# Gates and two parts of the short convolution by rows, norms spread through DRAM, and first loads on two queues

## The chip, the core and the metric

The kernel runs on one core of a Trainium2 chip. The core has five engines with an instruction queue each: TensorE (PE in the profile; its weight loads, PEld, overlap its matmuls), VectorE (DVE), ScalarE (ACT), GpSimd (POOL) and SyncE (SP). Each takes its own queue in order. DMA transfers are issued from the queues of SP, ACT and POOL. The metric is device time of one execution in microseconds, lower is better.

## What is computed

One block of a hybrid encoder on 256 tokens of width 2048, in float32: a norm, one projection w_in into four mixers (gated linear attention, an FFT mixer, long convolutions, a short convolution), their outputs normed and projected by w_out, then cross-attention to 256 memory tokens and a gated MLP of inner width 5632. Cut to what the change touches:

```python
def short_conv(u, w):
    up = jnp.pad(u, ((0, 0), (1, 1), (0, 0)))
    return up[:, :-2] * w[0] + up[:, 1:-1] * w[1] + up[:, 2:] * w[2]

def shortconv_mixer(u, conv_w):
    b, c, h = jnp.split(u, 3, axis=-1)
    return b * short_conv(c * h, conv_w)

def gla_mixer(q, k, v, g, lr, gk_w, gk_b, norm_g):
    ...
    o = rms_norm(o, norm_g) * jax.nn.silu(heads(g, GLA_DV))

def reference(...):
    mem_n = rms_norm(mem, mem_norm_g)
    h = rms_norm(x, norm_g[l, 0])
    q, k, v, g, lr, u_f, u_h, u_s = jnp.split(h @ w_in[l], split_at, axis=-1)
    y_a = gla_mixer(q, k, v, g, lr, ...)
    y_b = rms_norm(fnet_mixer(u_f), grp_norm_g[l, 0])
    y_c = rms_norm(hyena_mixer(u_h, ...), grp_norm_g[l, 1])
    y_d = rms_norm(shortconv_mixer(u_s, sc_conv_w[l]), grp_norm_g[l, 2])
    x = x + jnp.concatenate([y_a, y_b, y_c, y_d], axis=-1) @ w_out[l]
    x = x + cross_attention(rms_norm(x, norm_g[l, 1]), mem_n, w_xq[l], w_xkv[l], w_xo[l])
    x = x + swiglu(rms_norm(x, norm_g[l, 2]), w_gate_up[l], w_down[l])
```

## The kernel before

**Weights and precision.** All weights stream once from DRAM, as blocks of 128 x 128, sixteen to a slab of 1 MB, in the very order in which the matmuls use them. Each half slab (eight blocks) is split on the way: ScalarE casts it to the high part wh (line 104), VectorE subtracts it from the raw one and makes the low part wl (line 105). Activations are split the same way into 512 columns, 256 high and 256 low. A product is wh x (high, low) plus wl x high, all in the matrix engine's fast float32 form. `Stream.take` (from line 110) gives out the blocks and keeps two to three halves ready ahead; SP's queue loads the slabs (line 83). Before the very first slab is in, `st.after` hands out other loads between the slabs' pieces, one after each.

**Three forms of a product.** `gemm` with `mm` yields *features*: 128 output columns on the partitions and the 256 tokens along the free axis; a block costs a matmul of 512 columns (L298) and one of 256 (L299). Its two halves have to be added afterwards (`merge`, L305). The *narrow* form of `mm` takes three matmuls of 256 (L295, L296, L299) and needs no merge. `gemm_rows` with `part_rows` yields *rows*: tokens on the partitions, 512 output columns along the free axis; four blocks cost six matmuls of 512 (L347 to L349). What is computed by rows but wanted as features is turned: VectorE transposes blocks of 32 x 32 (`store_turned`, L382), POOL's queue stores them to DRAM, and `load_turned` (L389) reads them back so that rows and columns change places; the features then stand in a turned order, which the host puts into the weights that use them.

**Side work.** Everything but the big products is written as generators in `Background`. After each product step `poll` takes a step of those that are due by a count of PE time and of VectorE's debts; `yield` without a number pauses a generator by 1.3 us plus the debt, SOON by almost nothing, FAR by 18 us. `drain` forces a generator to its end at once. The instructions of each engine are put in order at build time by a planner, which can put an instruction ahead of others that were written earlier when it takes the engine to be free; `keep_place` forbids that.

**The stages around the change.** First the keys and values of memory, by rows, with memory's slices scaled as they arrive (`start_m`). Beside it `prepare` sums the squares of memory and x, gets the reciprocal root as a column (`rstd_cols`) and spreads it along the free axis: `rstd_end` scales an identity by it (L275), and a matmul with ones (L282) puts it on all partitions, copied to krs (L285). x's row rsx is used by `start_x`, which norms and splits x's slices (L204 and L200); memory's row rsm scales the attention's scores. After memory the filters of the long convolution are computed (`filters`, with `dft`, L1069). Then w_in: twelve feature columns for the long convolution, v by rows, k and q by features, the first three short convolution columns narrow, FNet by rows, the other nine short convolution columns by features, the four gates narrow. In the background GLA's `mix`, FNet's `mix` and the short convolution's `group_norm` go on. `out_proj` takes the inner dimension in four parts, the long convolution's, GLA's, the short convolution's and FNet's; ahead of each but the first it drains the generator concerned and issues loads of x for the residual. Attention and the MLP follow; the MLP's first Silu (L870) closes the first pair of gate and up.

Small tiles of 256 columns come from a pool of eleven (`tmp`); PSUM has four banks for the big products (pg) and four for side work (pm).

## Time and profile before

| | us |
|---|---|
| median of 3 runs | 1478.01 |
| lowest and highest | 1476.25 and 1478.46 |
| profiled execution, its own time | 1477.61 |
| its span, first to last instruction | 1475.6 |
| PE busy in the span | 1463.1 |
| VectorE, ScalarE, POOL busy | 930.6, 754.5, 152.9 |

The span's rest to the execution's time, 2.0 us, lies around it. In the rows that follow, a timeline row gives start, duration, engine, line and operation, output and input, and in brackets the engine's idle time before it with what ended it; starts and durations are in us from the span's start. The matmuls' durations are modelled and overlap, so a matmul of 512 columns shows 0.39 while the next starts 0.23 later.

### The profile page before, as it was taken

The numbers are of one execution on the slowest core, as the hardware profiler recorded it, in microseconds if no ns is written. First come the engines' busy times: TensorE is split into PE (matmuls) and PEld (weight loads), VectorE is DVE, ScalarE is ACT, GpSimd is POOL, SyncE is SP. The second block draws the span as 40 slices with busy tenths as digits, with TensorE's granted clock in tenths as the row PEclk, the third lists the DMA queues.
The fourth block names the chain that finished last, engine by engine and source line by source line (L and its number), as shares of the span: only waits on it lengthen the run. The fifth ranks groups of instructions, "written<-read, shape, count | busy, mean of one in ns | idle before, by whom it ended". The sixth has DMA issues, their size and how long they took to land.

```text
span 1475.6 us, 18641 instructions
## 1 busy us (share of the span) xinstructions
PE 1463.1 (99%) x7068; PEld 1227.5 (83%) x7068; DVE 930.6 (63%) x1336; ACT 754.5 (51%) x1104; POOL 152.9 (10%) x204
## 2 busy tenths in 40 slices
PE   9999999999999999999999999999999999999997
PEld 7887888898898888888888888888888888888886
DVE  6668768778777575886765554555555456444445
ACT  6557655467556463665544444444444445434344
POOL 0000100000001223420501100111100111000000
PEclk9999999999999999999999999999999999999999
DMA  9776655454536777764857666666666666555554
GB/s 355 272 282 243 208 206 171 145 182 168 200 129 205 232 260 236 248 190 143 260 197 218 207 216 214 227 215 217 226 214 206 215 219 229 189 186 195 199 198 144
DMA packets 57146, 312.33 MB, mean 212 GB/s; under 512 B 8381, under 2 KB 10078, under 8 KB 25440
## 3 DMA queue, kind: packets, MB, share of 16 engines
q1 hardware_dynamic: 46352, 281.11, 55.3%
q0 software_dynamic: 10272, 29.37, 7.3%
q8 instruction: 55, 0.90, 0.2%
q10 hardware_dynamic: 432, 0.66, 0.1%
q14 instruction: 35, 0.29, 0.1%
HBM read 294.33 MB, written 16.78 MB: 211 GB/s over the span
## 4 chain that ended last, share of the span: by engine, by line
PE 97%; DVE 1%; ACT 0%; DMA 0%; issue 0%; SPq 0%; DVEq 0%
PE pg L347 24%; PE pg L349 24%; PE pg L348 24%; PE pg L298 9%; PE pg L299 6%; PE pm L349 1%; PE pm L348 1%; PE pm L347 1%; PE pg L295 1%; PE pg L296 1%; PE pm L1069 1%; PE pm L843 1%; PE pm L815 0%; DMA raw<-in_W 0%; PE pm L1450 0%
## 5 line engine op out<-in xcount | busy, mean ns | idle before, releaser
L105 DVE TENSOR_TENSOR wl<-raw,wh 128x1024 fp32r<-128x1024 f32 (+2 forms) x505 | 611.6, 1213 | 464.3 <-ACT wh L104 462.9
L104 ACT CAST wh<-raw 128x1024 fp32r<-128x1024 f32 (+2 forms) x505 | 523.9, 1039 | 567.8 <-PE pg L349 469.3
L347 PE MATMUL pg<-wh,act 128*128 128x512 f32 (+1 forms) x1434 | 559.7, 390 | 1.6 <-ACT wh L104 1.2
L348 PE MATMUL pg<-wl,act 128*128 128x512 f32 (+1 forms) x1434 | 558.0, 389 | 0.6 <-DVE wl L105 0.5
L349 PE MATMUL pg<-wh,act 128*128 128x512 f32 (+1 forms) x1434 | 558.0, 389 | 0.0
L347 PEld LDWEIGHTS pg<-wh,act 128*128 128x128 f32 x1434 | 269.2, 188 | 59.8 <-ACT wh L104 1.8
L348 PEld LDWEIGHTS pg<-wl,act 128*128 128x128 f32 x1434 | 269.2, 188 | 56.6 <-DVE wl L105 1.4
L349 PEld LDWEIGHTS pg<-wh,act 128*128 128x128 f32 x1434 | 269.2, 188 | 56.1
L298 PE MATMUL pg<-act,wh 128*128 128x512 f32 x576 | 202.9, 394 | 0.0
L299 PE MATMUL pg<-act,wl 128*128 128x256 f32 x688 | 192.7, 280 | 0.0
L299 PEld LDWEIGHTS pg<-act,wl 128*128 128x128 f32 x688 | 129.4, 188 | 0.4
L298 PEld LDWEIGHTS pg<-act,wh 128*128 128x128 f32 x576 | 108.2, 188 | 23.5
L384 POOL DMA_DIRECT2D hidden<-u x22 | 16.7, 762 | 403.3 <-DVE u L382 403.3
L347 PE MATMUL pg<-wh,f 128*128 128x512 f32 x120 | 46.7, 389 | 0.0
L348 PE MATMUL pg<-wl,f 128*128 128x512 f32 x120 | 46.7, 389 | 0.0
L349 PE MATMUL pg<-wh,f 128*128 128x512 f32 x120 | 46.7, 389 | 0.0
L389 POOL DMA_DIRECT2D tmp<-hidden x44 | 38.8, 888 | 46.7 <-DMA hidden<-u 29.6
L295 PE MATMUL pg<-act,wh 128*128 128x256 f32 x112 | 31.7, 283 | 0.0
L296 PE MATMUL pg<-act,wh 128*128 128x256 f32 x112 | 31.4, 281 | 0.0
L389 POOL DMA_DIRECT2D mr<-keys x16 | 14.1, 888 | 152.2 <-DVE act L200 148.1
L348 PEld LDWEIGHTS pg<-wl,f 128*128 128x128 f32 x120 | 22.5, 188 | 4.7
L347 PEld LDWEIGHTS pg<-wh,f 128*128 128x128 f32 x120 | 22.5, 188 | 4.7
(311 smaller groups left out, 1198.4 us busy)
## 6 DMA issues: line engine op xcount, KB each, us to landing
raw<-in_W SPq DMA_DIRECT2D x246, 1024.0 KB, 5.0
raw<-in_W SPq DMA_DIRECT2D x11, 512.0 KB, 7.3
hidden<-u POOLq DMA_DIRECT2D x22, 256.0 KB, 3.6
tmp<-hidden POOLq DMA_DIRECT2D x44, 128.0 KB, 4.3
features<-tmp POOLq DMA_DIRECT2D x24, 128.0 KB, 3.2
res<-in_xT SPq DMA_DIRECT2D x5, 512.0 KB, 6.7
ar<-features POOLq DMA_DIRECT2D x20, 128.0 KB, 6.2
k<-in_mem SPq DMA_DIRECT2D x8, 256.0 KB, 8.4
```

The lines of the kernel that those rows point to most:

```text
L104: nc.scalar.copy(wh[:, a:b], r[:, a:b])
L105: nc.vector.tensor_tensor(out=wl[:, a:b], in0=r[:, a:b], in1=wh[:, a:b].bitcast(F32), op=ALU.subtract)
L295: self.nc.tensor.matmul(p[:, 0:R], wh, slot[:, 0:R], start=start, stop=False)
L296: self.nc.tensor.matmul(p[:, 0:R], wh, slot[:, R:512], start=False, stop=False)
L298: self.nc.tensor.matmul(p[:, :], wh, slot[:, :], start=start, stop=False)
L299: self.nc.tensor.matmul(p[:, 0:R], wl, slot[:, 0:R], start=False, stop=stop)
L347: self.nc.tensor.matmul(p, hi, wh, start=start, stop=False)
L348: self.nc.tensor.matmul(p, hi, wl, start=False, stop=False)
L349: self.nc.tensor.matmul(p, lo, wh, start=False, stop=stop)
L384: self.nc.gpsimd.dma_start(to[r], u.rearrange("p (k c) -> p k c", c=P))
L389: self.nc.gpsimd.dma_start(t.rearrange("p (g t) -> p g t", t=32), src)
L843: nc.tensor.matmul(p[:, :], vh[m][:, s], pt[m][:, :], start=m == 0, stop=False)
```

## The change

1. Gates and the parts c and h of the short convolution are computed by rows, 512 columns each, and their results (Silu of the gates, the product c x h) turned through DRAM by POOL's queue. Part b stays by features, now after the gates; no column is narrow any more. A new generator `short_conv` reads the products back, takes the taps, multiplies by b and norms.
2. FNet's projection moves ahead of them, into the stage before; `Fnet` is split into `__init__` and `open`.
3. `out_proj` takes FNet second, GLA third and the short convolution last.
4. `spread` replaces `rstd_end` for memory and x: POOL's queue stores the two columns to DRAM in token order, and a second transfer reads them back onto all partitions.
5. At the start, memory's slices 1 to 3 are issued from POOL's queue at once, instead of between the slabs' pieces on SP's.
6. One more `yield` ahead of each `dft` of the filters, and a Silu on one column in the MLP's `norm()`, kept in its place.
7. The host turns the weights, gains and taps that see the turned order.

```diff
@@ constants @@
-ROWS = ((0, 512), (704, 768), (880, 944), (1152, 1344), (1408, 1600), (1664, 1856), (1920, NBLK))
+ROWS = ((0, 512), (704, 768), (832, 1088), (1152, 1344), (1408, 1600), (1664, 1856), (1920, NBLK))
-NSC = 3
@@ -287,6 +285,15 @@
         return rest
+    def spread(self, y, pool):
+        n = next(self.kept)
+        d = self.nc.dram_tensor(f"spread{n}", (1, R), F32, kind="Internal").ap()
+        rs = pool.tile([P, R], F32, name=f"krs{n}")
+        self.nc.gpsimd.dma_start(d.rearrange("o (r p) -> p (o r)", p=P), y)
+        self.nc.gpsimd.dma_start(rs, d.partition_broadcast(P)[:, 0, :])
+        return rs
     def mm(self, p, w, k, c, slot, start, stop, narrow=False):
@@ -300,10 +307,10 @@
         self.bg.pe(0.353 if narrow else 0.346)
         self.bg.poll()
-    def merge(self, p):
+    def merge(self, p, u=None):
         t = self.tmp()
         self.nc.scalar.copy(t, p[:, R:512])
-        u = self.tmp()
+        u = self.tmp() if u is None else u
         self.tt(u, p[:, 0:R], t, ALU.add)
@@ -408,10 +415,11 @@
         self.xf = [self.outside(n, KT) for n in ("features1", "features2")]
         self.qf = self.outside("queries", KT)
+        self.sf, self.gf = self.outside("products", 4), self.outside("gates", 4)
         self.ff = self.outside("hidden", FT)
         self.vd = nc.dram_tensor("values", (P, 8 * 512), F32, kind="Internal").ap()
-        def load(src, k, n):
-            nc.sync.dma_start(self.res[k // 4][:, k % 4:k % 4 + n, :].rearrange("p k r -> p (k r)"),
+        def load(src, k, n, by=nc.sync):
+            by.dma_start(self.res[k // 4][:, k % 4:k % 4 + n, :].rearrange("p k r -> p (k r)"),
                               self.t[src][:, k * R:(k + n) * R])
@@ -423,8 +431,10 @@
         nc.vector.memset(self.eps, EPS)
         nc.scalar.copy(self.eps, self.eps)
-        st.after = [lambda: None, lambda: None]
-        st.after += [lambda a=a: load("memT", *a) for a in ((1, 1), (2, 1), (3, 1), (4, 1), (5, 1), (6, 2), (8, 2), (10, 2), (12, 2), (14, 2))]
+        for k in (1, 2, 3):
+            load("memT", k, 1, nc.gpsimd)
+        st.after = [lambda: None for _ in range(5)]
+        st.after += [lambda a=a: load("memT", *a) for a in ((4, 1), (5, 1), (6, 2), (8, 2), (10, 2), (12, 2), (14, 2))]
         st.after.append(lambda: nc.sync.dma_start(self.vec, self.t["vecs"]))
@@ -484,36 +494,33 @@
             self.rcm = self.rstd_cols(c[0][:, 0:2], D, self.cp)
             yield
-            rest = self.rstd_end(self.rcm, 0, self.cp)
-            yield
-            self.rsm = rest()
+            self.rsm = self.spread(self.rcm, self.cp)
             self.bg.add(hy.filters())
             nc.sync.dma_start(gl.lrw, self.t["lrw"])
             while not rows:
                 yield 3
             yield from squares("x", c[1])
-            rest = self.rstd_end(self.rstd_cols(c[1][:, 0:2], D), 0, mid)
-            yield
-            self.rsx = rest()
+            self.rsx = self.spread(self.rstd_cols(c[1][:, 0:2], D), mid)
         UF, UH, US = 1568, 2080, 3616
-        scols, cur = [], {}
-        for j in range(4):
-            scols += [US + 512 + j * P, US + 1024 + j * P, US + j * P]
-        def ev_s(i, p):
-            j, what = i // 3, i % 3
-            u = p[:, 0:R] if i < NSC else self.merge(p)
-            if what == 0:
-                cur["c"] = u
-                if i < NSC:
-                    cur["c"] = self.tmp()
-                    nc.scalar.copy(cur["c"], u)
-            elif what == 1:
-                self.tt(cur["c"], u, cur["c"], ALU.mult)
-                cur["y"] = self.conv3(cur["c"], V_SCW + 3 * j)
-            else:
-                self.tt(self.res[1][:, j, :], u, cur["y"], ALU.mult)
+        def short_conv(u0):
+            m = []
+            for k in range(4):
+                m.append(self.tmp())
+                self.load_turned(m[-1], self.sf, k)
+            yield FAR
+            for j in range(4):
+                m[j] = self.conv3(m[j], V_SCW + 3 * j)
+                yield
+            for j in range(4):
+                while len(u0) <= j:
+                    yield
+                y = self.res[1][:, j, :]
+                self.tt(y, y, m[j], ALU.mult)
+                yield SOON
+            yield from self.group_norm(self.res[1], 2, act[20:24])
         with tc.tile_pool(name="mid", bufs=1) as mid:
@@ -550,24 +557,41 @@
                     nc.scalar.copy(gl.v[r], p)
                 self.gemm("w_in", [256, 384, 0, 128], h, lambda i, p: gl.feed(i, self.merge(p)))
-                self.gemm("w_in", scols[0:NSC], h, ev_s, narrow=True)
+                fn = Fnet(self, act[20:24])
+                fn.feed(self.gemm_rows("w_in", [UF], h)[0])
                 self.bg.drain()
             with tc.tile_pool(name="glp", bufs=1) as glp:
                 gl.open(glp)
-                fn = Fnet(self, glp, act[20:24])
+                fn.open(glp)
                 g_gla = self.bg.add(gl.mix(act[4:8]))
-                fn.feed(self.gemm_rows("w_in", [UF], h)[0])
                 g_fn = self.bg.add(fn.mix(act[0:4], gl))
-                self.gemm("w_in", scols[NSC:], h, lambda i, p: ev_s(i + NSC, p))
-                g_sc = self.bg.add(self.group_norm(self.res[1], 2, act[20:24]), True)
-                def ev_gate(i, p):
-                    nc.scalar.activation(gl.gate[i], p[:, 0:R], AF.Silu)
-                self.gemm("w_in", [1024 + i * P for i in range(4)], h, ev_gate, narrow=True)
+                halves = [(r, j) for r in range(2) for j in range(0, 512, R)]
+                ps = self.gemm_rows("w_in", [US + 512], h)[0]
+                c = [self.tmp() for _ in halves]
+                for t, (r, j) in zip(c, halves):
+                    nc.scalar.copy(t, ps[r][:, j:j + R])
+                ps = self.gemm_rows("w_in", [US + 1024], h)[0]
+                for t, (r, j) in zip(c, halves):
+                    self.tt(t, ps[r][:, j:j + R], t, ALU.mult)
+                    self.store_turned(self.sf, j // P, r, self.tmp(), t)
+                u0 = []
+                g_sc = self.bg.add(short_conv(u0), True, True)
+                ps = self.gemm_rows("w_in", [1024], h)[0]
+                for r, j in halves:
+                    t = self.tmp()
+                    nc.scalar.activation(t, ps[r][:, j:j + R], AF.Silu)
+                    self.store_turned(self.gf, j // P, r, self.tmp(), t)
+                for k in range(4):
+                    self.load_turned(gl.gate[k], self.gf, k)
+                def ev_s(i, p):
+                    u0.append(i)
+                    self.merge(p, self.res[1][:, i, :])
+                self.gemm("w_in", [US + i * P for i in range(4)], h, ev_s)
                 gl.done = True
-                return self.out_proj(lambda n: self.bg.drain((g_gla, g_sc, g_fn)[n]))
+                return self.out_proj(lambda n: self.bg.drain((g_fn, g_gla, g_sc)[n]))
     def conv3(self, u, c, y=None):
@@ -675,7 +699,7 @@
             if n:
                 before(n - 1)
-                for c in ((2, 3), (1,), (0,))[n - 1]:
+                for c in ((0,), (2, 3), (1,))[n - 1]:
                     if c == 3:
@@ -684,7 +708,7 @@
         self.mix = act[4:8] + act[0:4] + act[16:24]
-        return self.gemm_rows("w_out", [0, 512], self.mix, parts=[range(k, k + 4) for k in (8, 0, 12, 4)], before=ready)
+        return self.gemm_rows("w_out", [0, 512], self.mix, parts=[range(k, k + 4) for k in (8, 4, 0, 12)], before=ready)
     def attention(self, ps):
@@ -893,6 +917,10 @@
                     yield pause
         def norm():
+            mark = self.mark()
+            nc.scalar.activation(self.mg[:, 0:1], self.mg[:, 0:1], AF.Silu)
+            self.keep_place(mark)
             yield 2.0
@@ -1164,6 +1192,7 @@
                     m.append(self.halves(d))
                     yield SOON
+                yield
                 self.dft(cs, m, self.sp[o][cs])
@@ -1418,8 +1447,11 @@
 class Fnet:
-    def __init__(self, b, pool, s):
+    def __init__(self, b, s):
         self.b, self.s = b, s
+    def open(self, pool):
+        b = self.b
         tile_ = lambda n, w: [pool.tile([P, w], F32R, name=n + x) for x in "hl"]
@@ kernel() @@
+    for a, n in ((V_GRP + 8, 4), (V_GLA, 1), (V_SCW, 12)):
+        vecs[:, a:a + n] = turned(vecs[:, a:a + n])
...
-    src["w_xq"][:, 1536:] = turned(src["w_xq"][:, 1536:].T).T
+    for n, a in (("w_xq", 1536), ("w_in", 512), ("w_in", 3616)):
+        src[n][:, a:a + 512] = turned(src[n][:, a:a + 512].T).T
+    for a in (0, 1536):
+        src["w_out"][a:a + 512] = turned(src["w_out"][a:a + 512])
```

More of the change, by code (lines that the diff above doesn't have):

```diff
@@ L1517 @@
     vecs[:, V_NG:V_NG + 48] = col(x["norm_g"])
-    for c in (16, 32):
-        vecs[:, V_NG + c:V_NG + c + 12] = turned(vecs[:, V_NG + c:V_NG + c + 12])
     vecs[:, V_GRP:V_GRP + 12] = col(x["grp_norm_g"])
@@ L1528 @@
     vecs[:, V_NT:V_NT + 2] = nt
+    for a, n in ((V_GRP + 8, 4), (V_GLA, 1), (V_SCW, 12)):
+        vecs[:, a:a + n] = turned(vecs[:, a:a + n])
+    for c in (16, 32):
+        vecs[:, V_NG + c:V_NG + c + 12] = turned(vecs[:, V_NG + c:V_NG + c + 12])
     gkw = np.zeros((32, 4, 2, 64), f32)
```

## The prediction

> **What bounds the kernel.** The profile's page comes first: whose busy time fills the span.
>
> ```profile
> span 1475.6 us, 18641 instructions
> ...
> PE 1463.1 (99%) x7068; PEld 1227.5 (83%) x7068; DVE 930.6 (63%) x1336; ACT 754.5 (51%) x1104; POOL 152.9 (10%) x204
> ```
>
> PE, the matrix engine, is idle for 12.5 us of 1475.6. So the time can fall in two ways only: less work for PE, or one of its few waits gone. It can rise without limit, by new waits. The busy time of each engine in windows of 20 us says where the idle 12.5 us lie (columns: window, its length, then PE, PEld, DVE, ACT and POOL, clock, DMA share, GB/s).
>
> ```profile
> 0.00:20.00 20.00, 17.18 (x79) 14.07 (x80) 11.99 (x23) 13.45 (x24) 0.70 (x6) 1.00 0.89 312
> ...
> 140.00:160.00 20.00, 20.00 (x89) 16.17 (x88) 18.99 (x30) 14.18 (x21) 2.15 (x4) 1.00 0.55 199
> ...
> 1460.00:1480.00 20.00, 7.72 (x35) 6.05 (x33) 3.69 (x12) 5.52 (x11) 0.00 (x0) 0.85 0.30 106
> ```
>
> The start loses 2.82 and the end 7.88 (15.6 less 7.72). Of the 1.8 left, three waits, whose rows stand below, make nearly all: two in the stage of the filters, one at the MLP's first gate; elsewhere PE is as full as in the middle row. The change touches all of these but the end.
>
> **Work of PE.** The timeline of PE gives the pace of each form by start times, which is safer than the modelled durations. Features, 512 and 256 columns a weight block:
>
> ```profile
> 299.64 0.39 PE L298 MATMUL pg<-act,wh 128*128 128x512 f32 x1
> ...
> 303.46 0.39 PE L298 MATMUL pg<-act,wh 128*128 128x512 f32 x1
> ```
>
> Eleven pairs lie between: 3.82 / 11 = 0.347 us a block. The narrow form, three times 256:
>
> ```profile
> 441.08 0.28 PE L295 MATMUL pg<-act,wh 128*128 128x256 f32 x1
> ...
> 445.35 0.28 PE L295 MATMUL pg<-act,wh 128*128 128x256 f32 x1
> ```
>
> Twelve triples: 4.27 / 12 = 0.356 a block. Rows, where six matmuls of 512 do four blocks:
>
> ```profile
> 353.62 0.39 PE L349 MATMUL pg<-wh,act 128*128 128x512 f32 x1
> ...
> 355.89 0.39 PE L347 MATMUL pg<-wh,act 128*128 128x512 f32 x1
> ```
>
> Ten matmuls: 0.227 each, so 6 x 0.227 / 4 = 0.3405 a block. Gates and short convolution are 16 groups of 128 columns by 16 slices, 256 blocks. Before, 112 are narrow and 144 features:
>
> ```profile
> L295 PE MATMUL pg<-act,wh 128*128 128x256 f32 x112 | 31.7, 283 | 0.0
> ```
>
> 112 x 0.356 + 144 x 0.347 = 89.84 us. After, 192 go by rows and the 64 of part b by features: 65.38 + 22.21 = 87.59. **Gain 2.25 us**, almost all of it certain: the same columns stream, in fewer instructions. FNet's projection is by rows in both; moved, it costs the same.
>
> The norms' spread by a matmul with ones leaves PE, two matmuls each for x and memory:
>
> ```profile
> 66.04 0.24 PE pm L282 x2
> ```
>
> 2 x 0.24 = **0.48 us**.
>
> **Waits that go.** The DFT of the filters issues on PE before VectorE has made the low halves (w3l); with one more yield ahead of it, a pause of at least 1.3 us in PE time stands there, more than either wait. The gate's Silu loads its table while PE's banks wait for it; the changed norm() loads it earlier, where weights lie ready ahead.
>
> ```profile
> 118.70 0.40 PE L1069 MATMUL pm<-w3h,tabh 128*128 128x512 f32 x1
> 119.56 0.50 PE L1069 MATMUL pm<-w3l,tabh 128*128 128x512 f32 x1 [0.47 <-DVE w3l L200]
> ...
> 120.13 0.40 PE L1069 MATMUL pm<-w3h,tabh 128*128 128x512 f32 x1
> 121.30 0.50 PE L1069 MATMUL pm<-w3l,tabh 128*128 128x512 f32 x1 [0.77 <-DVE w3l L200]
> ...
> 789.93 1.28 ACT L870 ACT_TABLE_LOAD   x1
> ...
> 791.16 0.39 PE L349 MATMUL pg<-wh,act 128*128 128x512 f32 x1
> 791.96 0.50 PE L347 MATMUL pg<-wh,act 128*128 128x512 f32 x1 [0.42 <-ACT g L870]
> ```
>
> From start to start, less the 0.227 of a matmul, they cost 0.63 + 0.94 = **1.57** and **0.57 us** (the modelled end hides 0.16 of each idle time). The 1.28 of the table is longer than 0.57, so all of that goes. At worst the DFT only waits elsewhere: 0 for the 1.57.
>
> **The start.** Three slices of memory leave SP's queue for POOL's. In the chain of waits and the timeline:
>
> ```profile
> 2.14 0.43 SPq L414 DMA_DIRECT2D res<-in_memT  x1
> 2.61 6.87 DMA raw<-in_W
> ...
> 8.88 0.39 PE L349 MATMUL pg<-wh,act 128*128 128x512 f32 x1
> 10.17 0.49 PE L347 MATMUL pg<-wh,act 128*128 128x512 f32 x1 [0.90 <-ACT wh L104]
> ```
>
> The weights of slice 1, issued at 2.61, land at 9.48, and PE loses 1.29 - 0.23 = 1.06 us there. After, they are issued in the place of the memory slice, at 2.14, 0.47 earlier, and 128 KB fewer stand ahead of them on SP. At best the whole idle 2.82 of the first window goes; at worst POOL's 384 KB move first, 256 KB more than now: at the 312 GB/s of that window 0.82 us later, less the 0.47, so 0.35 lost. I take **0.5 gained**, the earlier issue alone. Behind the three loads POOL has only the identity, which nobody reads in this window.
>
> **The spread through DRAM** is the one added wait I fear. For memory the result is first read in the attention:
>
> ```profile
> L200 DVE TENSOR_TENSOR tmp<-tmp,krs x8: 424/426/427, 603.3 to 675.8; 128x256 f32<-128x256 f32 x8
> ```
>
> From 603.3 us on, so it is free. For x, the rows are these (issues: count, KB, median us to landing, the first from 120 to 150 us, the second from 490 to 560).
>
> ```profile
> 128.11 0.16 DVE L204 SCALAR_TENSOR_TENSOR rc<-rc 128x2 f32<-128x2 f32 x1
> ...
> 133.30 0.36 ACT L285 COPY krs<-pm 128x256 f32<-128x256 f32 x1
> 135.76 2.06 DVE L204 SCALAR_TENSOR_TENSOR res<-res,vec,krs 128x256 f32<-128x256 f32 x5
> ...
> 153.18 1.21 DVE L105 TENSOR_TENSOR wl<-raw,wh 128x1024 fp32r<-128x1024 f32 x1
> ...
> 157.73 0.39 PE L348 MATMUL pg<-wl,act 128*128 128x512 f32 x1
> ```
>
> ```profile
> values<-tmp POOLq DMA_DIRECT2D x7, 128.0 KB, 2.4
> ...
> ar<-features POOLq DMA_DIRECT2D x8, 128.0 KB, 7.1
> ...
> k<-in_mem SPq DMA_DIRECT2D x8, 256.0 KB, 8.4
> ```
>
> The columns are done at 128.27. Store and load-back take 2.4 + 2.4 to 2.4 + 7.1, so the row is there between 133.1 and 137.8. The multiplications with it stand early in VectorE's order, at 135.76, long before the projection that needs them: if the row is late, VectorE stands still up to 2.0 us, and behind it the halves wl for PE. How much PE has in hand: the wl done at 154.39 is, counted off half by half, first used at 157.73, 3.3 us, the least of the busy stretch that follows (18.99 of 20 us). So 2.0 is absorbed: **0**, bounds 0 and, below, 6 to 14. POOL's own queue, held by the load-back, has only the stores of values behind it, which are 20 us apart.
>
> [...]
>
> **VectorE, ScalarE and buffers from 340 to 460 us.** Five merges go (an add on VectorE and a copy on ScalarE each), eight transposes come.
>
> ```profile
> L382 DVE STREAM_TRANSPOSE tmp<-res 128x256 f32<-128x256 f32 x12 | 4.3, 414 | 0.0
> ...
> 406.31 1.23 DVE L105 TENSOR_TENSOR wl<-raw,wh 128x1024 fp32r<-128x1024 f32 x1 [1.10 <-ACT wh L104]
> ...
> 414.11 2.36 DVE L105 TENSOR_TENSOR wl<-raw,wh 128x1024 fp32r<-128x1024 f32 x2
> ```
>
> An add taken like a transpose, 3 x 0.414 = 1.2 us more on an engine with room. What matters is the burst: products, four multiplications and four transposes in one go, 8 x 0.414 = 3.3 us. PE has borne more: between two wl at 406.31 and 414.11 lie 7.8 us, and that window shows no idle PE. The round trip of the products (2.4 + 7.1) fits into the pause of 18 us ahead of the taps; the gates have the 22 us of part b. **0**; if a transpose waits for a buffer whose store is still landing, 3.3 + 2.4 is still under the 7.8. FNet's projection ahead only moves its VectorE work out of the stage of GLA's gates.
>
> **The end of the mixers.** The short convolution now ends last, and its norm must be through when the out-projection comes to it as its fourth part, before as the third. A part is 4 x 2 x 6 x 0.227 = 10.9 us, so it has 32.7 us from its last column.
>
> ```profile
> 436.41 0.42 DVE L200 TENSOR_TENSOR res<-tmp 128x256 f32<-128x256 f32 x1
> ...
> 475.23 1.67 DVE L204 SCALAR_TENSOR_TENSOR res<-res,vec,rs 128x256 f32<-128x256 f32 x4 [0.39 <-ACT rs L285]
> ...
> 477.96 1.43 DVE L200 TENSOR_TENSOR act<-res,act 128x256 fp32r<-128x256 f32 x4
> ```
>
> Before, the last product of the short convolution stands at 436.41, and of the two norms that follow, its own and FNet's, the later is split at 479.4: up to 43.0 us. That was in turn with FNet's norm and GLA's four; now FNet's is through before, so I take it to fit: **0**. If it doesn't, what is left is forced at once with PE waiting; multiplications and splits, from 475.23 to 479.4, are 4.2 us. The loads of x for the residual stand behind these drains on SP's queue as before, in another order.
>
> **Sum.** 2.25 + 0.48 + 1.57 + 0.57 + 0.5 = 5.37, from which I take 0.3 for small new waits, since three such arose in this kernel already: 5.1. The profiled execution took 1477.61 us, 2.0 round its span, and lies 0.4 under the median 1478.01. From the median: 1478.0 - 5.1 = **1472.9**.
>
> **Rivals.**
>
> First, the queues at the start compete, and the weights of slice 1 come 0.35 later instead of earlier: 1472.9 + 0.85 = 1473.8. For it: the window moves 312 GB/s already. Against: bytes after them on SP were moved before they landed, so there is room to reorder. [...]
>
> Second, the norm of the short convolution is late for its part, and PE waits the 4.2 us: 1477.1, no change that shows. For it: 43.0 against 32.7. Against: fewer norms take turns.
>
> Third, **slower**: the row of x comes so late that VectorE stands still beyond PE's stock. It decides from 3.3 us after 135.76, at 139.1. With both legs at the 8.4 of the longest row the row comes at 145.1, PE loses 9.3 - 3.3 = 6.0: 1478.9. [...] I put 1481.5. For it: nothing holds the multiplications back in the order. Against: the order may put them where the row is expected.
>
> **How the numbers follow.** Forecast 0.55, its own range 1470.6 to 1475; first rival 0.14, second 0.15, third 0.16. About 0.2%, 3.0 us, can be told from no change; so faster means under 1475.05, slower over 1481.0. Forecast and first rival give 0.69 of faster, less 0.02 for the forecast's upper edge: 0.67. The second gives no change, with these 0.02 and 0.05 of the third: 0.22. The rest of the third: 0.11. The range begins at 1470.3, where the start gains 2.8 instead of 0.5 and nothing new arises, and goes to 1479.2, which leaves out the worse half of the third.
>
> **What would show it.** PE's sum of idle time falls from 12.5 to about 10; no wait on w3l and on the gate; no table load ahead of the first gate; rows in place of narrow matmuls; the krs row's first reader not idle for more than 2 us. I am wrong if PE has an idle microsecond between 128 and 170, or behind a transpose between 340 and 460, or where the fourth part of the out-projection begins, or waits longer than before for the second slice's weights.

## The result, and the profile after

The changed kernel takes 1500.7 us (median of 6 runs, 1500.04 to 1504.23), the kernel before 1476.34 in the same batch (6 runs, 1475.89 to 1478.46): ratio 1.0168, 95% interval 1.0155 to 1.0181. It is 24.4 us slower, where 5.1 faster was predicted, and outside the range. The profiled execution took 1504.23, the slowest of the six, with a span of 1502.2; so the trace holds some 2 us more of loss than the medians (the two spans differ by 26.6). The page of the changed kernel:

```profile
span 1502.2 us, 18260 instructions
...
PE 1469.6 (98%) x6856; PEld 1223.1 (81%) x6856; DVE 930.7 (62%) x1335; ACT 755.8 (50%) x1099; POOL 170.5 (11%) x227
```

PE is idle for 32.6 us instead of 12.5. It is also busy for 6.5 us more, although it does less work; why, the clock will show. The waits of PE, in the view that sums them by what ended them (us in total, times, longest):

```profile
PE pg L355 <- DVE wl L103: 8.6, 4, 7.4
PE pm L1129 <- DMA k<-in_c: 5.0, 1, 5.0
PE pm L1482 <- DVE fal L198: 4.2, 1, 4.2
PE pm L1170 <- DVE w3l L198: 3.3, 1, 3.3
PE pg L354 <- ACT wh L102: 2.4, 2, 2.1
```

Nearly all of it is a few long stops, and each has its place in PE's timeline:

```profile
11.77 0.50 PE L354 MATMUL pg<-wh,act 128*128 128x512 f32 x1 [2.07 <-ACT wh L102]
...
72.22 1.11 PE L1129 MATMUL pm<-k 33*64 33x256 f32 x2 [5.00 <-DMA k<-in_c]
...
158.12 0.79 PE L355 MATMUL pg<-wl,act 128*128 128x512 f32 x1 [7.43 <-DVE wl L103]
163.03 0.79 PE L1170 MATMUL pm<-w3l,hs 128*128 128x512 f32 x1 [3.27 <-DVE w3l L198]
...
393.17 0.79 PE L1482 MATMUL pm<-fal,fch 128*128 128x512 f32 x1 [4.19 <-DVE fal L198]
...
832.27 0.50 PE L355 MATMUL pg<-wl,act 128*128 128x512 f32 x1 [0.76 <-DVE wl L103]
```

Behind a long stop the matmuls themselves are slower. Windows of the changed kernel, with the columns of the prediction's (the last three: clock, DMA share, GB/s):

```profile
0.00:20.00 20.00, 16.10 (x65) 13.24 (x66) 11.30 (x22) 12.23 (x22) 2.48 (x9) 0.91 0.87 287
...
72.00:76.00 4.00, 3.78 (x9) 2.45 (x10) 3.46 (x6) 2.55 (x4) 0.00 (x0) 0.50 0.92 381
76.00:80.00 4.00, 4.00 (x16) 3.26 (x15) 3.79 (x9) 1.47 (x2) 0.00 (x0) 0.83 0.76 258
...
140.00:160.00 20.00, 12.33 (x50) 9.29 (x49) 4.47 (x9) 8.28 (x11) 0.56 (x1) 0.90 0.71 146
...
392.00:396.00 4.00, 2.83 (x7) 2.25 (x8) 3.87 (x9) 0.42 (x3) 0.00 (x0) 0.50 0.00 0
```

From 72 to 76 us the granted clock is 0.50, and PE counts as almost fully busy with 9 instructions where it does some 17 at full clock. So a stop costs its length and then some: of the stops below, 7.1 us for 5.00 idle at 67 us, 13.3 for 7.43 and 3.27 near 158, 6.7 for 4.19 at 389, which is 2.1 to 2.6 more. Counted from start to start, less what the matmuls take at full clock, and against the kernel before, the stops make:

| stop of the changed kernel | us lost against before |
|---|---|
| start, weights of slice 1 | 3.2 |
| 67 us, filters' k from in_c | 7.1 |
| 150 to 166 us, wl and w3l | 13.3 |
| 389 us, FNet's second DFT | 6.7 |
| 831 us, weights behind the MLP's first gates | 1.0 |

Together 31.3. Less the 4.87 that the prediction took for rows (2.25), the ones' matmuls (0.48), the DFT's waits (1.57) and the gate's Silu (0.57), this gives 26.4, where the two spans differ by 26.6. So the gains seem to have come, and the losses are five stops. The waits on w3l near 120 us and ahead of the MLP's second row product are gone; so is the table load ahead of the gate; there are no narrow matmuls.

What stands behind the two largest is in POOL's, VectorE's and ScalarE's timeline:

```profile
50.52 0.74 POOL L293 DMA_DIRECT2D spread<-krc  x1 [46.91 <-DVE krc L202]
60.01 0.56 POOL L294 DMA_DIRECT2D krs<-spread  x1 [8.76 <-DMA spread<-krc]
...
138.39 0.71 POOL L293 DMA_DIRECT2D spread<-rc  x1 [2.53 <-DVE rc L202]
149.37 0.56 POOL L294 DMA_DIRECT2D krs<-spread  x1 [10.27 <-DMA spread<-rc]
...
153.31 0.62 ACT L214 CAST w3h<-k 128x512 fp32r<-128x512 f32 x1 [7.24 <-DMA k<-in_c]
...
156.05 0.88 DVE L202 SCALAR_TENSOR_TENSOR res<-res,vec,krs 128x256 f32<-128x256 f32 x2 [15.53 <-DMA krs<-spread]
```

The store of one kilobyte takes 9.2 and 10.7 us to land. VectorE stands 15.5 us on the row of x; but ScalarE stands too, on a load that has nothing to do with the row. The windows of 52 to 62 us, first of the kernel before, then of the changed one, say what the store does to others:

```profile
52.00:62.00 10.00, 10.00 (x45) 8.27 (x45) 6.54 (x9) 4.04 (x4) 1.91 (x3) 1.00 0.97 346
```

```profile
52.00:62.00 10.00, 10.00 (x46) 8.29 (x45) 7.02 (x9) 4.19 (x4) 1.99 (x3) 1.00 0.74 29
```

346 GB/s before, 29 after, with the DMA engines still counted 0.74 busy: they are occupied and move almost nothing.

### The profile page after: what moved, and what is told of

It reads as the page before. It is cut to its first block, busy times and chain, and to the rows that moved or that the text cites. A ratio compares the mean times of both kernels' runs of the same rounds, so it can differ in the third digit from the quotient of the medians.

```text
span 1502.2 us, 18260 instructions
## 1 busy us (share of the span) xinstructions
PE 1469.6 (98%) x6856; PEld 1223.1 (81%) x6856; DVE 930.7 (62%) x1335; ACT 755.8 (50%) x1099; POOL 170.5 (11%) x227
## 4 chain that ended last, share of the span: by engine, by line
PE 88%; issue 6%; DMA 2%; DVE 1%; ACT 1%; POOL 1%; SPq 0%; POOLq 0%; ACTq 0%; DVEq 0%
PE pg L354 23%; PE pg L355 23%; PE pg L356 23%; PE pg L305 8%; PE pg L306 4%; PE pm L355 1%; PE pm L356 1%; PE pm L354 1%; PE pm L1097 1%; DMA spread<-krc 1%; DMA raw<-in_W 1%; PE pm L867 1%; PE pm L839 0%; DMA krs<-spread 0%; POOL keys L391 0%
## 5 line engine op out<-in xcount | busy, mean ns | idle before, releaser
L355 PE MATMUL pg<-wl,act 128*128 128x512 f32 (+1 forms) x1530 | 598.4, 391 | 8.6 <-DVE wl L103 8.6
L354 PE MATMUL pg<-wh,act 128*128 128x512 f32 (+1 forms) x1530 | 600.4, 392 | 2.4 <-ACT wh L102 2.4
L356 PE MATMUL pg<-wh,act 128*128 128x512 f32 (+1 forms) x1530 | 598.0, 391 | 0.0
L355 PEld LDWEIGHTS pg<-wl,act 128*128 128x128 f32 x1530 | 288.9, 189 | 69.2 <-DVE wl L103 10.0
L354 PEld LDWEIGHTS pg<-wh,act 128*128 128x128 f32 x1530 | 289.2, 189 | 65.5 <-ACT wh L102 3.2
L356 PEld LDWEIGHTS pg<-wh,act 128*128 128x128 f32 x1530 | 288.8, 189 | 60.5
L305 PE MATMUL pg<-act,wh 128*128 128x512 f32 x496 | 174.4, 394 | 0.0
L306 PE MATMUL pg<-act,wl 128*128 128x256 f32 x496 | 138.8, 280 | 0.0
L306 PEld LDWEIGHTS pg<-act,wl 128*128 128x128 f32 x496 | 93.2, 188 | 0.3
L391 POOL DMA_DIRECT2D features<-tmp x24 | 17.3, 723 | 80.7 <-DVE tmp L389 80.7
L354 PEld LDWEIGHTS pg<-wh,f 128*128 128x128 f32 x120 | 22.5, 188 | 4.7
L356 PEld LDWEIGHTS pg<-wh,f 128*128 128x128 f32 x120 | 22.5, 188 | 4.6
L198 DVE TENSOR_TENSOR act<-tmp,act 128x256 fp32r<-128x256 f32 x44 | 17.2, 418 | 5.0 <-ACT act L206 4.6
```

The source lines that it names most:

```text
L198: self.nc.vector.tensor_tensor(out=out, in0=a, in1=b, op=op)
L305: self.nc.tensor.matmul(p[:, :], wh, slot[:, :], start=start, stop=False)
L306: self.nc.tensor.matmul(p[:, 0:R], wl, slot[:, 0:R], start=False, stop=stop)
L354: self.nc.tensor.matmul(p, hi, wh, start=start, stop=False)
L355: self.nc.tensor.matmul(p, hi, wl, start=False, stop=False)
L356: self.nc.tensor.matmul(p, lo, wh, start=False, stop=stop)
```

## The experiments

Twelve kernels. Every time is beside runs of the kernel before on the same chip; differences between batches are taken through it.

**x1_no_spread.** Both norms by the ones' matmul again (`rstd_end`), the rest as changed.

```diff
-            self.rsm = self.spread(self.rcm, self.cp)
+            rest = self.rstd_end(self.rcm, 0, self.cp)
+            yield
+            self.rsm = rest()
...
-            self.rsx = self.spread(self.rstd_cols(c[1][:, 0:2], D), mid)
+            rest = self.rstd_end(self.rstd_cols(c[1][:, 0:2], D), 0, mid)
+            yield
+            self.rsx = rest()
```

> Both norms are spread by the matmul with ones again, all else as in the changed kernel. Theory (the store in four-byte pieces holds the transfers and, for x, VectorE): PE's stop at 66.8 us (5.2 us and 1.9 us of slow clock behind it) and the one at 150.3 us (13.3 us with its slow clock) are gone, the two at the start and at 388 us stay: 1500.7 - 20.4 + 0.5 for the ones' matmuls = 1480.8 us. Rival (the stops come from the filters and other background work standing earlier in the order): both stops stay, 1499 to 1502 us.

1483.65 (before 1477.59; ratio 1.0041, 1.0026 to 1.0056). The changed kernel was 24.4 over before, this one is 6.1 over: the spread costs **18.3 us** of it, net of the 0.48 of the ones' matmuls. The stop at 67 us is gone, and of the 13.3 around 150 us 0.3 are left. The start, FNet's DFT and the place near 808 (ScalarE 6.96 on tmp from hidden) stay.

**x2_spread_128B.** The columns are turned on VectorE first, so that the store goes in pieces of 128 bytes.

```diff
-        self.nc.gpsimd.dma_start(d.rearrange("o (r p) -> p (o r)", p=P), y)
+        a, b = (pool.tile([P, 64], F32, name=f"{x}{n}") for x in ("spa", "spb"))
+        self.nc.gpsimd.memset(a, 0.0)
+        self.nc.vector.tensor_copy(a.rearrange("p (r i) -> p r i", r=2)[:, :, 0], y)
+        self.nc.vector.transpose(b, a)
+        for r in range(2):
+            self.nc.gpsimd.dma_start(d[0, r * P:(r + 1) * P].rearrange("(q i) -> q i", q=4), b[0:P:32, r * 32:(r + 1) * 32])
```

> The spread through DRAM stays, but VectorE turns the columns first, so that the store goes in pieces of 128 bytes instead of four. Theory (piece size): the store lands within some 4 us instead of 8.8 and 10.3, the throughput of the other transfers does not fall to nothing beside it, and at least 15 of the 20.4 us of the two stops go: 1480 to 1486 us. Rival (any round trip through DRAM is too long for the order in which VectorE has its work): VectorE still waits 10 us or more for the row of x, 1490 to 1500 us.

1486.98 (ratio 1.0057, 1.0041 to 1.0074), 9.4 over before, just outside the expected range. The DMA view of x's spread and VectorE's timeline (issues: count, KB, median us to landing):

```profile
spread<-spb POOLq DMA_DIRECT2D x2, 0.5 KB, 3.0
...
krs<-spread POOLq DMA_DIRECT2D x1, 128.0 KB, 5.3
```

```profile
140.63 1.67 DVE L202 SCALAR_TENSOR_TENSOR res<-res,vec,krs 128x256 f32<-128x256 f32 x4 [7.18 <-DMA krs<-spread]
```

The same bytes land in 1.6 us (memory's) and 3.0 (x's), and the stop at 67 us is gone. But VectorE reaches the first multiplication 7.2 us before the row is back, and PE stops 4.1 us on w3l behind it, 7.0 with the rest. So there are two costs: the pieces, and the reader that stands too early even for this shorter round trip of 8.3 us.

**y3_mults_kept_in_place.** The stores in four-byte pieces stay; the multiplications by the row may not be put ahead of earlier work.

```diff
             x = self.resk(n)
+            mark = self.mark()
             self.stt(x, x, self.gvec(V_NG, n), self.rsx, ALU.mult, ALU.mult)
+            self.keep_place(mark)
```

> The changed kernel, where the multiplications by x's row keep their place in VectorE's order, behind the work written ahead of them; both stores stay as they are. It parts the two ways in which x's store can cost at 150 us. Theory one: VectorE's stand of 15.5 us on the row is what stops the halves wl for PE; without it the stop shrinks to what is left of ScalarE's 7.2 us wait for k from in_c less PE's stock of 3.3, so 8 to 12 us are won: 1489 to 1493. Theory two: the starved transfers are the cause, whoever stands first: PE still stops 7 us or more near 150, 1497 to 1501.

1491.04 (before 1477.13; ratio 1.0091, 1.0075 to 1.0106): 13.9 over before, 10.5 less than the changed kernel, as theory one forecast. The loss around 150 shrinks from 13.3 to some 5.5; what is left is not VectorE's:

```profile
148.78 0.62 ACT L214 CAST w3h<-k 128x512 fp32r<-128x512 f32 x1 [7.63 <-DMA k<-in_c]
```

The stop at 67 us shrank as well, from 7.1 to 3.4, and nothing in the edit explains this. k came as late after its issue (15.3 us) as in the changed kernel (15.4), but SP issued it at 54.76 instead of 56.93; why is left open. So of the 10.5 only some 7.8 at 150 count for the reader.

**y2_memory_by_ones.** Memory's row by the matmul, x's by the store.

```diff
-            self.rsm = self.spread(self.rcm, self.cp)
+            rest = self.rstd_end(self.rcm, 0, self.cp)
+            yield
+            self.rsm = rest()
```

> The changed kernel with memory's norm spread by the matmul with ones again; x's row is still stored in four-byte pieces. Theory: the stop at 66.8 us (7.1 us with the slow clock behind it) is made by memory's store alone, and the one at 150 by x's store alone, so the first goes and the second stays: some 7 us under the changed kernel, 1493 to 1494. Rival: the loads that came late at 60 us were late for another reason (the filters' loads moved together), then 1500 with the stop still there.

1496.43 (ratio 1.0131, 1.0115 to 1.0146): 5.1 under the changed kernel, less than expected, partly, it seems, because the start lost 4.1 against before in this trace and 3.2 in that one. The stop at 67 us is gone, the one at 145 (9.92 on w3l) stays. Each stop belongs to its store.

**z3_stores_unread and z4_stores_unread_act.** These go on from y4_best below. Both stores come back, but nobody reads them; the rows come from the ones' matmul. In z3 POOL issues them, in z4 ScalarE (`self.nc.scalar`).

```diff
+    def store_row(self, y):
+        n = next(self.kept)
+        d = self.nc.dram_tensor(f"spread{n}", (1, R), F32, kind="Internal").ap()
+        self.nc.gpsimd.dma_start(d.rearrange("o (r p) -> p (o r)", p=P), y)
...
+            self.store_row(self.rcm)
             rest = self.rstd_end(self.rcm, 0, self.cp)
...
+            col = self.rstd_cols(c[1][:, 0:2], D)
+            self.store_row(col)
+            rest = self.rstd_end(col, 0, mid)
```

> y4_best with the two stores in four-byte pieces put back on POOL's queue, their results not read by anyone (the rows come from the matmul with ones). It measures what such a store does to the transfers beside it, with no reader late. Theory: it stalls the loads on SP's queue for 9 to 11 us each time; PE stops at 66 us for k from in_c as in the changed kernel (3.4 to 7.1 us with the slow clock), and at 145 us by some 3 to 5: 7 to 12 us over y4_best, 1481 to 1486. Rival: the load-back of 128 KB onto all partitions is what the loads wait for, or the late row alone: then under 2 us over y4_best, 1474 to 1476.

> z3_stores_unread with the two stores on ScalarE's DMA queue instead of POOL's. Theory: the pieces of four bytes are the cause, whatever queue they come from: the same stops, 1481 to 1486. Rival: it is POOL's queue with its descriptors made by software that holds the others up; then the stores are as short from ScalarE's queue as other small transfers (some 2 us), and the time is y4_best's, 1473 to 1475.

1483.26 (ratio 1.0043, 1.0028 to 1.0059) and 1483.1 (1.0043, 1.0029 to 1.0057), 6.3 and 6.2 over before where y4_best is 3.3 under: **9.6 and 9.5 us for two kilobytes that no one waits for**. The store of memory's column in z3's view of issues, with the window of its flight, then the same window of y4_best, then the store and its window in z4:

```profile
spread<-krc POOLq DMA_DIRECT2D x1, 1.0 KB, 8.5
```

```profile
47.00:55.00 8.00, 8.00 (x37) 6.64 (x36) 6.51 (x9) 3.35 (x4) 3.38 (x5) 1.00 0.77 30
```

```profile
47.00:55.00 8.00, 8.00 (x37) 6.60 (x37) 6.51 (x8) 3.15 (x3) 3.14 (x4) 1.00 0.76 253
```

```profile
spread<-krc ACTq DMA_DIRECT2D x1, 1.0 KB, 8.6
```

```profile
46.00:55.00 9.00, 9.00 (x41) 7.47 (x40) 7.51 (x9) 4.18 (x6) 3.15 (x4) 1.00 0.72 42
```

It is as long from ScalarE's queue and empties the other queues as much. So it is the pieces, not POOL's queue. That the two sums agree to 0.1 is in part luck: z4 loses 1.2 at 67 us, where z3 loses 4.3, but also 2.0 near 120 us on w3l, which z3 doesn't lose and which isn't shown to come of the store. PE pays later, at the loads that were held up (z3, both places):

```profile
68.83 0.64 PE L1139 MATMUL pm<-k 33*64 33x256 f32 x2 [2.65 <-DMA k<-in_c]
...
151.97 0.71 PE L1179 MATMUL pm<-w3h,hs 128*128 128x512 f32 x1 [4.16 <-ACT w3h L214]
```

**x3_start_one_queue.** Memory's slices 1 to 3 on SP's queue again, between the slabs' pieces.

```diff
-        for k in (1, 2, 3):
-            load("memT", k, 1, nc.gpsimd)
-        st.after = [lambda: None for _ in range(5)]
+        st.after = [lambda: None, lambda: None]
```

> Memory's slices 1 to 3 go back to SP's queue, between the slabs' pieces, all else as in the changed kernel. Theory (the loads of the two queues share the engines, so the weights of slice 1 land 1.6 us later and PE falls to the slow clock): the first 20 us are 3.2 us shorter, 1497.5 us. Rival (the loss at the start lies in the run, not in the queues): 1500.7 us.

1499.64 (ratio 1.0149, 1.0134 to 1.0164), 22.1 over before: 2.3 less than the changed kernel, though by the two intervals this alone is not certain. The traces say more. Counted as in the table, against the kernel before, PE loses 0.9 to 4.1 us in the first 30 with three slices on POOL's queue (the changed kernel, 3.2, and five kernels here); with one queue it is between 1.4 won and 0.3 lost (seven kernels). In the chain of waits of the changed kernel the weights of slice 1 stand as

```profile
2.14 8.94 DMA raw<-in_W
```

where the kernel before had 2.61 and 6.87.

**x4_fnet_later.** FNet's side work starts 30 us later, so that GLA's scans are through VectorE first.

```diff
-        yield
+        yield 30.0
         for h in range(2):
```

> FNet's side work begins 30 us of PE time later, as it did in the kernel before; its projection stays ahead, all else as in the changed kernel. Theory (its first DFT takes turns with GLA's gates on VectorE and PE waits in order for the low half): the stop at 388 us, 4.35 us and 2.3 us of slow clock, is gone, 1494.0 us. Rival (the stop comes from the load of the gates alone): PE waits elsewhere between 370 and 410 us, 1499 to 1502 us.

A miss: 1512.61 (ratio 1.0232, 1.0215 to 1.0249), 10.7 worse than the changed kernel. The stop at FNet's DFT goes, but the end of the mixers comes late, and the out-projection forces what is left:

```profile
PE pg L354 <- ACT act L206: 5.8, 2, 3.0
...
PE pm L1397 <- ACT gkr L1388: 3.1, 1, 3.1
```

The two of the first line stand at 500 and 527 us, ahead of the second and the fourth part. Behind each of these stops the clock is low again: 0.50 from 432 to 440 us, 0.57 from 500 to 504, 0.96 in the mean from 528 to 560. This is the prediction's second rival, made by hand: here the slack of the norms isn't 30 us.

**y4_best.** Norms by ones' matmuls, one queue at the start, and 6 us of pause in the one place where it is wanted.

```diff
+            yield 6.0
             p = b.bank()
             for c in range(2):
                 triple(p, [x[:, c * P:(c + 1) * P] for x in self.c], [x[:, c * 512:(c + 1) * 512] for x in self.a], c == 0, c == 1)
```

> The changed kernel without its three costly parts: both norms by the matmul with ones, memory's first slices on SP's queue again, and 6 us of pause ahead of FNet's second DFT so that PE doesn't come to it before VectorE's fal. What is left is rows (2.25), the yield (1.57) and the Silu (0.57), 4.4 us, less up to 2.5 at the MLP's first gates: 1472 to 1475 where the kernel before has 1476.3, interval below 1. Rival: the stop at FNet's second DFT only moves to another place (the end of the mixers, as in x4_fnet_later), then 1477 to 1481.

1473.84 (before 1477.13; ratio 0.9977, 0.9968 to 0.9986). No stop at FNet's DFT, none between 405 and 560. What is left is 1.03 at the MLP's first gates: ScalarE stands 5.75 on tmp from hidden ahead of three casts of weights:

```profile
798.86 0.41 ACT L206 CAST act<-tmp 128x256 fp32r<-128x256 f32 x1 [5.75 <-DMA tmp<-hidden]
```

**z2_fnet_old_place.** y4_best with FNet's projection back behind GLA's opening, without the pause.

```diff
-                fn = Fnet(self, act[20:24])
-                fn.feed(self.gemm_rows("w_in", [UF], h)[0])
                 self.bg.drain()
...
+                fn = Fnet(self, act[20:24])
                 fn.open(glp)
                 g_gla = self.bg.add(gl.mix(act[4:8]))
+                fn.feed(self.gemm_rows("w_in", [UF], h)[0])
```

> y4_best with FNet's projection back behind GLA's opening, ahead of the part c, and without the 6 us of pause ahead of FNet's second DFT. It asks whether the projection's earlier place made the stop of 4.1 to 4.4 us at the second DFT. Theory: yes; with the projection between, GLA's scans are through VectorE before fal is due, no stop between 340 and 405 us, and the time is y4_best's, 1472.5 to 1475 (ratio 0.9965 to 0.9985). Rival: the stop comes of what took the projection's place in general (rows in place of narrow columns take merges and pauses away, so side work is drawn in faster): then the stop is still there, 5.7 to 6 us: 1478 to 1480 (ratio 1.001 to 1.002).

1480.61 (before 1476.94; ratio 1.0028, 1.0018 to 1.0039). Against the theory, PE still stops there:

```profile
365.34 0.50 PE L1484 MATMUL pm<-fah,fch 128*128 128x512 f32 x1 [2.36 <-ACT fah L214]
```

With the slow clock behind it (0.50 from 366 to 368 us) this place loses some 4.6, where the changed kernel lost 6.7, and 2.4 are lost near 805. The rival came, at 0.6 over its range. So the projection's place is not the whole cause. What goes with the stop is how far FNet's first DFT is behind the second matmul of GLA's gates: 349.54 to 380.00 in the kernel before, 30.5 us, no stop; 341.35 to 355.86 here, 14.5; 378.68 to 380.94 in the changed kernel, 2.3. In between lie GLA's exponentials on ScalarE and scans on VectorE, which the casts and halves of FNet have to pass. Why the distance isn't 30 us with the projection at its old place was not tried.

**y1_before_yield_silu.** The kernel before with the more yield and the early Silu alone.

```diff
         def norm():
+            mark = self.mark()
+            nc.scalar.activation(self.mg[:, 0:1], self.mg[:, 0:1], AF.Silu)
+            self.keep_place(mark)
             yield 2.0
...
+                yield
                 self.dft(cs, m, self.sp[o][cs])
```

> The kernel before, with edit 6 alone: the one more yield ahead of each DFT of the filters, and the Silu on one column in the MLP's norm(). Theory: both edits do what they are for, PE's waits on w3l (1.57) and on the gate's Silu (0.57) go, 2.1 us together, so the time is 2.1 us under the kernel before of the same batch (1474.2 where before is 1476.3), with an interval below 1. Rival: the Silu put early reorders ScalarE's work around the MLP's norm, and the stop at the MLP's first gates that the changed kernel shows (ScalarE 5.5 us on the DMA of tmp from hidden, PE's excess 1.0 there; 2.5 in x1_no_spread) is of its making; then 1.0 to 2.5 us come back: between 1.1 under and 0.4 over the kernel before.

1474.69 (before 1477.13; ratio 0.9982, 0.9974 to 0.9991): 2.4 us won, 2.14 forecast. ScalarE does wait longer on tmp from hidden here too (first before, then y1):

```profile
803.51 0.41 ACT L208 CAST act<-tmp 128x256 fp32r<-128x256 f32 x1 [2.00 <-DMA tmp<-hidden]
```

```profile
799.98 0.41 ACT L208 CAST act<-tmp 128x256 fp32r<-128x256 f32 x1 [4.65 <-DMA tmp<-hidden]
```

It comes to this split 6.2 us earlier (795.33 against 801.51): behind the first Silu the planner now puts three casts of weights ahead of it, four before, while the slice lands only 3.5 earlier. PE loses nothing that shows.

**z1_best_later_hidden.** y4_best, with the MLP's first split of a hidden slice later.

```diff
                 if k >= k0 + ahead:
+                    if k == ahead:
+                        yield 6.0
                     mark = self.mark()
```

> y4_best with 6 us more of pause ahead of the MLP's first split of a hidden slice. In y4_best ScalarE stands 5.75 us on tmp from hidden there and PE loses 1.03. Theory: the split was put ahead of the weights' casts before its slice was back from DRAM; later, nothing stands, 1.0 us won: 1472.8 where y4_best had 1473.8 and before 1477.1 (ratio 0.997). Rival: the split stays early in ScalarE's order or the stand comes back at the next slices: 1473.8 (ratio 0.9977).

1471.92 (before 1476.94; ratio 0.9969, 0.9957 to 0.9980), the fastest here: 5.0 us under the kernel before. ScalarE waits 0.49 in place of 5.75:

```profile
801.41 0.41 ACT L206 CAST act<-tmp 128x256 fp32r<-128x256 f32 x1 [0.49 <-DMA tmp<-hidden]
```

In y4_best PE's longest wait there was 0.76; here none is left. Over y4_best it is 1.7 by the batches, where 1.0 was expected; the two intervals overlap, so the size isn't certain.

## Why the prediction was wrong

The step that failed is **the spread through DRAM, put at "0, bounds 0 and, below, 6 to 14"**, and in it three things. Two of the prediction's own signs of being wrong came: an idle PE between 128 and 170 us, and a longer wait for the second slice's weights.

- *Memory's spread "is free"*, since the row is read at 603 us. I priced only the reader. The store itself held the loads of the filters, and PE lost 7.1 at 67 us. z3 shows that no reader is needed.
- *The first leg at 2.4 us*, from the stores of values. Those are 128 KB in rows; this is 1 KB in 256 pieces, and it landed in 9.2 and 10.7. For x the legs together took 17.4 (10.7 and 6.7), not 9.5. The 14 of the bounds, and with it the third rival's 1481.5, count with a first leg of twice 8.4 us. That was my estimate and no run shows the term; the runs show a first leg of 8.5 to 10.7.
- *"VectorE stands still up to 2.0 us"*, absorbed by PE's stock of 3.3. The stand was 15.5. Besides the long legs, the reader came nearer: the prediction left it where it stood in the kernel before, 7.5 us behind the finished column (128.27 to 135.76). In the changed kernel it stands 2.4 behind (138.10 to 140.52, that is 156.05 less the stand), in x2 4.3. So with x2's short legs of 3.0 and 5.3 us the reader still stood 7.2. The third rival had this mechanism; it got 0.16, and its price of 6 to 14 was right for x alone. That 15.5 less the stock of 3.3 is 12.2, close to the 13.3 that PE lost, is in part luck: the 13.3 holds the slow clock and the late k, and without VectorE's stand y3 still loses 5.5 there.

Both spreads cost 18.3 us (x1_no_spread), of which the stores alone make 9.6 (z3_stores_unread, measured on y4_best); the rest, if the two add up, is x's early reader and the load-back (some 7.8 at 150 us go with the reader in y3_mults_kept_in_place).

**The start, "0.5 gained".** The issue at 2.14 came as forecast; the landing took 8.94 instead of 6.87, at 11.08 instead of 9.48, and with the low clock behind it (0.63 from 12 to 14 us, 0.52 from 14 to 16) 3.2 were lost. The first rival had the sign; its bound of 0.35, three slices' bytes over the window's rate, was too small. Bytes alone don't give the delay.

**FNet's projection "only moves its VectorE work out of the stage of GLA's gates".** False: FNet's mix now ran into the exponentials and scans of GLA's gates, and PE lost 6.7 us at its second DFT. I looked for the projection's own adds and not for what its generator issues next, which has to come out of the same two engines. z2 limits this: with the projection back, 4.6 of the 6.7 remain, so its place accounts for some 2.1 at most. The removed narrow columns ahead of GLA may have their part in the rest; this is argued, not shown.

**The "0.3 for small new waits"** covers the 1.0 at the MLP's first gates badly. The early Silu has its part: y1, which changes nothing else there, has the same order of three casts and then the split. But in y1 PE loses nothing by it, so the Silu alone doesn't make the 1.0.

**What held.** The DFT's yield and the Silu: 2.14 forecast, 2.4 measured alone (y1). Rows in place of narrow and features: 2.25 forecast; z1_best_later_hidden is 5.0 under before, y1 2.4, which leaves 2.6 for rows and what goes with them. The 0.48 of the ones' matmuls was never measured by itself. The bursts of transposes and the end of the mixers, both at 0: PE is busy 40.00 of 40 us in each window from 400 to 560 of the changed kernel, so the second rival didn't come, until x4 forced it. Rows, yield and Silu together were forecast at 4.4, and z1_best_later_hidden measures 5.0, with an interval of 3.0 to 6.4; this kernel, which keeps them and leaves out the rest reaches 1471.9.

## What to carry to other kernels

Ask of a transfer not only when it is read but what it keeps from moving: beside a store in pieces of four bytes the core moved 29 to 42 GB/s here instead of 253 and 346, so turn a column first (x2_spread_128B: 3.0 us to landing instead of 10.7) or spread it on an engine. When a value goes through DRAM, fix its reader's place in the order behind the round trip. When a product is moved, follow the side work that it releases to the engines that it then shares, and price a stop of PE with the low clock behind it on top, which was 2.1 to 2.6 us for the three longest of the changed kernel.

## What the hardware showed

**A kilobyte in four-byte pieces.** From POOL's queue the 256 pieces of memory's column took 8.5 us to land in z3_stores_unread, 9.0 in y3_mults_kept_in_place, 9.2 in the changed kernel and 9.4 in x3_start_one_queue, x's in the changed kernel 10.7; from ScalarE's queue memory's took 8.6 (z4_stores_unread_act). Beside memory's store the core moved 29 to 42 GB/s, with the DMA engines counted 0.72 to 0.77 busy; without such a store it moved 346 (the kernel before, 52 to 62 us) and 253 (y4_best, 47 to 55 us). Beside x's store the rate falls as low only in the last part of the flight, in the changed kernel from 145 us on:

```profile
145.00:149.00 4.00, 4.00 (x19) 3.27 (x19) 0.00 (x0) 1.05 (x1) 0.00 (x0) 1.00 0.66 59
```

The changed kernel's DMA records have the store of memory's column as 16 packets of 64 bytes, each under 0.05 us and all begun by 52.02 us. It is the loads' own packets of 8 KB that become slow: of those begun between 52 and 62 us the median takes 3.41 us, in the kernel before 0.31. Why, stays open. Nor do the runs part the number of pieces from their size (256 of 4 bytes, 8 of 128), or from their all going to one kilobyte of DRAM.

**The clock after a stop.** Behind the stop at 67 us in the changed kernel PE's matmuls start 0.43 apart instead of 0.227, for 4 us:

```profile
73.85 0.63 PE L355 MATMUL pg<-wl,act 128*128 128x512 f32 x1
74.28 0.63 PE L356 MATMUL pg<-wh,act 128*128 128x512 f32 x1
...
77.27 0.46 PE L354 MATMUL pg<-wh,act 128*128 128x512 f32 x1
77.56 0.40 PE L355 MATMUL pg<-wl,act 128*128 128x512 f32 x1
```

A low clock followed PE's idle times of 2.07, 3.27, 4.19, 5.00 and 7.43 us in the changed kernel, 2.36 in z2_fnet_old_place, 2.65 and 4.16 in z3_stores_unread, 2.82 to 3.10 in x4_fnet_later and 3.23 in y3_mults_kept_in_place. It did not follow those of 0.76 in the changed kernel, 1.11 in z4_stores_unread_act and 1.18 in z1_best_later_hidden, where the windows behind show 1.00. In between it went either way at the same length, after 1.79 us in y3_mults_kept_in_place, then after 1.80 in z4_stores_unread_act:

```profile
70.00:72.00 2.00, 2.00 (x6) 1.59 (x5) 1.51 (x4) 2.00 (x4) 0.00 (x0) 0.50 1.03 434
```

```profile
150.00:152.00 2.00, 2.00 (x11) 1.65 (x10) 0.00 (x1) 0.30 (x1) 0.00 (x0) 1.00 0.57 236
```
